# Score sums in four column groups on 32-token blocks, and a rearranged start, in a two-layer HGRN2/Fourier kernel

## The chip, the cores and the metric

One core of a Trainium2 chip runs the whole program in one launch. The metric is the device time in microseconds (us), as the median over runs. The engines are PE (matrix multiply; the profile calls its weight loads PEld), DVE (vector), ACT (activation), POOL (general) and SP, which here only issues DMAs. Matmuls read SBUF and write PSUM; DVE and ACT read both.

## The reference, cut to what matters

512 latent tokens and 256 context tokens of width 1024 go through two layers. Layer 0 is a bidirectional gated linear recurrence with 16 heads of 128 channels:

```
h = rms_norm(x, norm_g) * (1 + scale) + shift          # shift, scale: silu(c) @ ada_w + ada_b
q = silu(p[0]);  f = lb + (1 - lb) * sigmoid(p[1:3])   # forward and backward gates
k = 1 - f;  g = log(f);  v = p[3];  z = p[4]           # p = h @ w_in, per head
scores[t, s] = sum_c q[t, c] * exp(b[t, c] - b[s, c]) * k[s, c]   for s <= t,  b = cumsum(g)
o[t] = sum_s scores[t, s] v[s] + (q[t] * exp(b[t])) @ S           # S: the state before the chunk
y = rms_norm(o_forward + o_backward) * silu(z) @ w_out
```

Layer 1 is a Fourier mixer, and a final norm ends the program. The change touches only the start of layer 0 and, of the scores, two parts in each head: the entries with s = t ("own") and those of the other token of a pair, s = t ^ 1 ("near"). Both are sums over the 128 channels of a product that DVE has made for each token: `ks` for own, `pn` for near.

## The kernel before, in words

**Precision.** Large products are made of three fp32r matmuls, hi*hi, lo*hi and hi*lo (`mm3`, lines 95 to 97). `split` (lines 56 and 57) makes the two parts: ACT copies to fp32r, DVE subtracts. Small matmuls (transposes, scores, states) are plain fp32, which the profile records as two instructions each.

**Start (lines 100 to 323).** SP issues, one after the other, `ident`, `vecs`, the gate bounds, the four tiles of `x` (`xs`, 512 KB each), then the eight modulation tiles (`ada_load(d)`: two halves `wa` of 512 KB each) with the first projection weights between them. `normalize(n)` scales a row tile: ACT squares and sums, POOL raises to -0.5, DVE multiplies. For each of eight channel tiles d: `ada_mm` multiplies `wa` by the two padded condition columns (`rp`), eight fp32 matmuls whose weights have 32 columns, so that four of them write four different groups of 32 PSUM partitions; ACT copies the result (`row`); `turn` transposes the rows (`tp`); `ada_cols` turns `row` into columns (`mp`), DVE adds biases (`acol`, `bcol`), and `modulate` makes `hlh` and `hll`, the two parts of h. Between these stand `product`s: the first head's four latent projections (`first`), as far as h and the weights are there. The order on PE, ACT and DVE in this part is the order of the code. After the eight steps the context rows are normalized, turned and modulated into `hc` in the same way, with the fourth projection between them.

**Heads (lines 332 to 605).** `projections` yields in the middle of each projection; at each yield `advance` moves the scan of the head before by one step, so that PE has projection matmuls (`pf`, `pq`, `pfc`, `vps`) between the steps of a scan. From here on a scheduler sets each engine's order. A scan has seven levels with block length h = 1, 2, 4 ... 64. At level `lev` PE multiplies `kk` by `z4` for four token tiles (`gp`, line 529), DVE then multiplies `z4` by the decays of that level (line 537, two instructions), ACT packs the next `kk` (line 492), and DVE writes the level's entries from `gp` into the score matrix `am` under a mask (line 553). At level 6 ACT copies two 64-row blocks instead (lines 550 and 551). After the levels `am` is the weight of the matmuls that make the head's output.

The two parts that change: `parts` splits `ks` and `pn` into hi and lo (ACT and DVE), and `summed` multiplies each by a 128x128 matrix of ones on PE, two fp32r matmuls of 512 columns, which gives every PSUM partition the sum of every token. DVE multiplies the first by the identity into `am` (line 543) at level 1, and copies the second under the mask of level 0 (line 546) at level 2. PSUM tiles of scores come from a pool of two buffers (`psG`).

Of the kernel before, what the change touches and what calls it, by code (L numbers as in the profile page):

```python
# [7 lines left out]
F32 = mybir.dt.float32  # L8
# [6 lines left out]
P = 128  # L15
D = 1024
KT = D // P
T = 512
# [14 lines left out]
def hgrn_fourier_kernel(ctx: ExitStack, tc: tile.TileContext, a):  # L33
# [77 lines left out]
    def ada_load(d):  # L111
        wa[d] = []
        for j in range(2):
            h = KT // 2
            if d < 4:
                w = py.tile([P, h, 256], F32, tag=f"yp{2 * d + j}", name=f"wa{d}_{j}")
            else:
                w = p0.tile([P, h, 256], F32, name=f"wa{d}_{j}")
            nc.sync.dma_start(out=w, in_=a["ada_a"][d][:, j * h:(j + 1) * h, :])
            wa[d].append(w)  # L120

    for n in range(NT):
        nc.sync.dma_start(out=xs[:, n, :], in_=a["x"][n * P:(n + 1) * P, :])
    ada_load(0)
    masks = pc.tile([P, 7, P], U8, name="masks")
    ones = pc.tile([P, 256], F32, name="ones")
# [5 lines left out]

    vp = psM("vp")
# [26 lines left out]
    lp = psM("lp")  # L160
    pe.transpose(lp[:, :32], lmx, ident[:32, :32])
    lbc = pc.tile([P, 32], F32, name="lbc")
    v.tensor_copy(lbc, lp[:, :32])
    omlb = pc.tile([P, 32], F32, name="omlb")
    v.tensor_scalar(out=omlb, in0=lbc, scalar1=-1.0, scalar2=1.0, op0=ALU.mult, op1=ALU.add)
# [112 lines left out]
    with tc.manual_schedule(engines={mybir.EngineType.PE, mybir.EngineType.Activation, mybir.EngineType.DVE}):  # L278
# [17 lines left out]
        for n in range(NTC):  # L296
            nc.sync.dma_start(out=xs[:, NT + n, :], in_=a["ctx"][n * P:(n + 1) * P, :])
        for n in range(NT):
            normalize(n)
        todo = {2: [(0, 0), (1, 0)], 3: [(0, 1), (1, 1), (2, 0), (2, 1)]}  # L300
        for d in range(KT):
            ada_mm(d)
            turn(d, 0)
            for j, k in todo.get(d, [(j, d - 2) for j in range(3)] if d > 3 else []):
                product(j, k)
            ada_cols(d)
            modulate(d, 0)
            if d < 3:
                W.halves(d)
        W.halves(3)  # L310
        for j in range(3):
            product(j, KT - 2)
        for n in range(NT, NT + NTC):
            normalize(n)
        for j in range(3):
            product(j, KT - 1)
        for d in range(KT):
            turn(d, 1)
            modulate(d, 1)
            product(3, d)  # L320
    mraw = p0.tile([P, 7, P], F32, tag="junk", name="mraw")
    nc.sync.dma_start(out=mraw, in_=a["masks"])
    g.tensor_copy(masks, mraw)

# [128 lines left out]
    def scan(i, fl, z4, fc, q, zs):  # L453
# [42 lines left out]
        def parts(pr, name):  # L496
            hi = pw.tile([P, T], F32R, tag="yh", name=f"{name}h{i}", bufs=2)
            lo = pw.tile([P, T], F32R, tag="yh", name=f"{name}l{i}", bufs=2)
            split(hi, lo, pr)
            return hi, lo  # L500

        def summed(hl, name):
            gp = psG(f"{name}p{i}")
            pe.matmul(gp, ones_r, hl[0], start=True, stop=False)
            pe.matmul(gp, ones_r, hl[1], start=False, stop=True)
            return gp.rearrange("p (n t) -> p n t", n=NT)
# [15 lines left out]
        for lev in range(7):  # L522
# [17 lines left out]
            if lev == 0:  # L540
                own = parts(ks, "gd")
            elif lev == 1:
                v.tensor_tensor(out=am, in0=summed(own, "gd"), in1=ident.unsqueeze(1).broadcast_to([P, NT, P]), op=ALU.mult)
                near = parts(pn, "gn")
            elif lev == 2:
                v.copy_predicated(am, level_mask(0), summed(near, "gn"))
            if lev > 0:
                g3 = gp.rearrange("p (n t) -> p n t", n=NT)
                if lev == 6:
                    s.activation(am[:64, :, 64:], g3[:64, :, 64:], AF.Copy)  # L550
                    s.activation(am[64:, :, :64], g3[64:, :, :64], AF.Copy)
                else:
                    v.copy_predicated(am, level_mask(lev), g3)  # L553
# [425 lines left out]
```

## Time and profile before

| | us |
|---|---|
| median of 3 runs | 1215.77 |
| lowest, highest | 1214.56, 1216.39 |
| the profiled execution's own time | 1213.96 |
| its span in the trace | 1212.2 |
| PE busy in the span | 1181.1 (97%) |
| DVE, ACT busy | 801.0 (66%), 548.8 (45%) |
| PE on the chain that ended last | 92% |
| DMA mean | 98 GB/s |

The span is cut into stages roughly so: start to 66 us, heads to 860 us, then the output projection of layer 0, the second layer and the end. A row of the page's list of groups gives line, engine, operation, tiles and shapes, then busy time and mean duration of one in ns, then the idle time of the engine before them and what ended it. A row of the timeline gives start, duration from the first to the last of merged instructions, engine, line, operation, tiles and count; in brackets the idle time before it and what ended it. PE's durations are modelled with overlap, so that the distance from start to start is what a matmul costs in a stream.

### The profile page before, as it was taken

The numbers are of one execution on the slowest core, as the hardware profiler recorded it, in microseconds if no ns is written. First come the engines' busy times: TensorE is split into PE (matmuls) and PEld (weight loads), VectorE is DVE, ScalarE is ACT, GpSimd is POOL, SyncE is SP. The second block draws the span as 40 slices with busy tenths as digits, with TensorE's granted clock in tenths as the row PEclk, the third lists the DMA queues.
The fourth block names the chain that finished last, engine by engine and source line by source line (L and its number), as shares of the span: only waits on it lengthen the run. The fifth ranks groups of instructions, "written<-read, shape, count | busy, mean of one in ns | idle before, by whom it ended". The sixth has DMA issues, their size and how long they took to land.

```text
span 1212.2 us, 18500 instructions
## 1 busy us (share of the span) xinstructions
PE 1181.1 (97%) x7450; PEld 1052.4 (87%) x7450; DVE 801.0 (66%) x1292; ACT 548.8 (45%) x1040; POOL 35.3 (3%) x69
## 2 busy tenths in 40 slices
PE   5989999999999999999999999999999999999997
PEld 3689899899889989989988988997888998988885
DVE  5484766786686586687658557558676856668554
ACT  4455444554453453445445345355556533333322
POOL 1000000000000000000000000000000000000000
PEclk9999999999999999999999999999999999999999
DMA  9411222232331332242221121113545313333221
GB/s 357 183 36 53 70 71 87 91 102 70 104 110 52 118 105 87 69 128 86 68 70 53 38 66 54 36 53 105 166 174 180 102 52 127 114 108 122 87 87 69
DMA packets 33671, 118.49 MB, mean 98 GB/s; under 512 B 3879, under 2 KB 4144, under 8 KB 33586
## 3 DMA queue, kind: packets, MB, share of 16 engines
q1 hardware_dynamic: 33586, 117.32, 29.7%
q8 instruction: 58, 0.95, 0.3%
q14 instruction: 27, 0.22, 0.1%
HBM read 115.20 MB, written 2.10 MB: 97 GB/s over the span
## 4 chain that ended last, share of the span: by engine, by line
PE 92%; DMA 3%; DVE 2%; ACT 1%; issue 1%; POOL 0%; SPq 0%; DVEq 0%; POOLq 0%; ACTq 0%
PE gp L529 7%; PE pq L95 5%; PE pq L96 5%; PE pq L97 5%; PE pf L95 4%; PE pf L97 4%; PE pf L96 4%; PE vps L97 4%; PE vps L95 4%; PE vps L96 4%; PE pfc L95 3%; PE pfc L96 3%; PE pfc L97 3%; PE o0a L97 2%; PE o0a L95 2%; PE o0a L96 2%
## 5 line engine op out<-in xcount | busy, mean ns | idle before, releaser
L57 DVE TENSOR_TENSOR wl<-wr,wh 128x1024 fp32r<-128x1024 f32 x140 | 170.6, 1219 | 99.9 <-ACT wh L56 99.8
L56 ACT ACTIVATE wh<-wr 128x1024 fp32r<-128x1024 f32 x140 | 148.0, 1057 | 177.7 <-issue 53.3
L537 DVE TENSOR_TENSOR z<-z,tt 128x512 f32<-128x512 f32 x192 | 123.8, 686 | 85.0 <-PE gp L529 81.6
L529 PE MATMUL gp<-z,kk 128*128 128x128 f32 x768 | 102.8, 277 | 2.1 <-ACT kk L492 1.9
L529 PEld LDWEIGHTS gp<-z,kk 128*128 128x128 f32 x768 | 97.8, 191 | 6.8 <-ACT kk L492 2.9
L95 PE MATMUL pf<-hlh,wh 128*128 128x512 f32 x240 | 97.6, 407 | 0.0
L95 PE MATMUL pq<-hlh,wh 128*128 128x512 f32 x240 | 97.0, 404 | 0.0
L492 ACT ACTIVATE kk<-z 128x512 f32<-128x512 f32 x96 | 61.8, 643 | 72.1 <-DVE z L537 72.0
L97 PE MATMUL pf<-hlh,wl 128*128 128x512 f32 x240 | 94.3, 393 | 0.0
L97 PE MATMUL pq<-hlh,wl 128*128 128x512 f32 x240 | 93.8, 391 | 0.0
L96 PE MATMUL pf<-hll,wh 128*128 128x512 f32 x240 | 93.8, 391 | 0.0
L96 PE MATMUL pq<-hll,wh 128*128 128x512 f32 x240 | 93.7, 390 | 0.0
L95 PE MATMUL pfc<-hc,wh 128*128 128x256 f32 x256 | 74.3, 290 | 3.0 <-ACT fl L402 3.0
L95 PE MATMUL vps<-wh,hlh 128*128 128x256 f32 x256 | 73.5, 287 | 0.0
L96 PE MATMUL pfc<-hc,wh 128*128 128x256 f32 x256 | 72.4, 283 | 0.0
L97 PE MATMUL vps<-wh,hll 128*128 128x256 f32 x256 | 72.4, 283 | 0.0
L96 PE MATMUL vps<-wl,hlh 128*128 128x256 f32 x256 | 72.4, 283 | 0.0
L97 PE MATMUL pfc<-hc,wl 128*128 128x256 f32 x256 | 72.4, 283 | 0.0
L553 DVE COPY_PREDICATED am<-masks,gp 128x512 f32<-128x512 uint8 x80 | 58.8, 735 | 0.3
L348 DVE SCALAR_TENSOR_TENSOR acc<-ar,scol,acc 128x1024 f32<-128x1024 f32 x30 | 38.5, 1283 | 26.3 <-DMA ar<-ada_r 26.2
L97 PEld LDWEIGHTS pf<-hlh,wl 128*128 128x128 f32 x240 | 45.1, 188 | 10.1 <-issue 0.2
L97 PEld LDWEIGHTS pq<-hlh,wl 128*128 128x128 f32 x240 | 45.0, 188 | 9.8
(267 smaller groups left out, 3019.5 us busy)
## 6 DMA issues: line engine op xcount, KB each, us to landing
wr<-hg_w SPq DMA_DIRECT2D x64, 512.0 KB, 3.5
ar<-ada_r SPq DMA_DIRECT2D x32, 512.0 KB, 3.7
wr<-ft_w SPq DMA_DIRECT2D x32, 512.0 KB, 3.8
wr<-hg_wout SPq DMA_DIRECT2D x29, 512.0 KB, 3.5
wa<-ada_a SPq DMA_DIRECT2D x16, 512.0 KB, 10.4
wr<-hg_v SPq DMA_DIRECT2D x16, 512.0 KB, 3.5
wr<-ft_wout SPq DMA_DIRECT2D x16, 512.0 KB, 3.5
xs<-x SPq DMA_DIRECT2D x4, 512.0 KB, 4.5
```

Of the source, the lines that this page charges most:

```text
L56: s.activation(hi, src, AF.Copy)
L57: v.tensor_tensor(out=lo, in0=src, in1=hi.bitcast(F32), op=ALU.subtract)
L95: pe.matmul(out, lh, rh, start=first, stop=False)
L96: pe.matmul(out, lh, rl, start=False, stop=False)
L97: pe.matmul(out, ll, rh, start=False, stop=last)
L348: v.scalar_tensor_tensor(out=acc, in0=raw, scalar=scol[:, 0, k:k + 1], in1=acc, op0=ALU.mult, op1=ALU.add)
L492: s.activation(view(kk, 0, [[2 * h, T // (2 * h)], [h, 2], [1, h]]), view(z4, 2 * T, [[2 * h, T // (2 * h)], [T + h, 2], [1, h]]), AF.Copy)
L529: pe.matmul(gp[:, n * P:(n + 1) * P], kk[:, n * P:(n + 1) * P], view(z4, n * P, dims), start=True, stop=True)
L537: v.tensor_tensor(out=za, in0=za, in1=ta, op=ALU.mult)
L553: v.copy_predicated(am, level_mask(lev), g3)
```

## The change

Three parts of the start and one of the heads:

- `ada_load(0)` is issued ahead of the four tiles of `x`. `ada_mm(0)` stands ahead of the rows' normalization, and 26 fp32r matmuls of ones by ones (`keep_warm`), whose results nobody reads, are put around it on PE. The gate bounds (`lp`) move behind the second `ada_mm`.
- The context rows are normalized in steps 6 and 7 of the loop instead of behind it; their transposes are issued two steps ahead, the first two ahead of the last nine products.
- Two small masks are made on POOL (`own_m`, `near_m`, 128x32: the sum of a 128x128 mask's four column blocks).
- In each head `sums` replaces `parts` and `summed`: for each of `ks` and `pn` four fp32 matmuls with 32 columns of ones as weights. The j-th takes the j-th block of 32 tokens of each of the four token tiles (128 columns) and writes PSUM partitions 32j to 32j+31, so that partition p holds the sums of the 32 tokens of p's own block. DVE masks these into `amc` (128 x 4 x 32; one multiplication and one copy under a mask), ACT copies four blocks of 32 partitions into `am`. No split is needed. Besides, level 5's copy under a mask on DVE becomes four copies of 32x128 elements on ACT.

```
+    ada_load(0)
     for n in range(NT):
         nc.sync.dma_start(out=xs[:, n, :], in_=a["x"][n * P:(n + 1) * P, :])
-    ada_load(0)
...
+    def keep_warm(n, name):
+        wp = psG(name)
+        for j in range(n):
+            pe.matmul(wp, ones_r, view(ones_r, 0, [[0, 4], [1, P]]), start=True, stop=True)
+
+    keep_warm(4, "warm0")
...
+        keep_warm(12, "warm1")
+        ada_mm(0)
+        keep_warm(10, "warm2")
         for n in range(NT):
             normalize(n)
...
-        W.halves(3)
+            if d > 5:
+                normalize(NT + d - 6)
         for j in range(3):
             product(j, KT - 2)
-        for n in range(NT, NT + NTC):
-            normalize(n)
+        W.halves(3)
+        for d in range(2):
+            turn(d, 1)
         for j in range(3):
             product(j, KT - 1)
         for d in range(KT):
-            turn(d, 1)
             modulate(d, 1)
             product(3, d)
+            if d + 2 < KT:
+                turn(d + 2, 1)
...
-        def summed(hl, name):
-            gp = psG(f"{name}p{i}")
-            pe.matmul(gp, ones_r, hl[0], start=True, stop=False)
-            pe.matmul(gp, ones_r, hl[1], start=False, stop=True)
-            return gp.rearrange("p (n t) -> p n t", n=NT)
+        def sums(srcs):
+            gp = psG(f"cs{i}")
+            for e, src in enumerate(srcs):
+                for j in range(4):
+                    pe.matmul(gp[32 * j:32 * j + 32, e * P:(e + 1) * P], ones[:, :32],
+                              view(src, 32 * j, [[P, NT], [1, 32]]), start=True, stop=True)
+            return [view(gp, e * P, [[32, NT], [1, 32]]) for e in range(2)]
...
-            if lev == 0:
-                own = parts(ks, "gd")
-            elif lev == 1:
-                v.tensor_tensor(out=am, in0=summed(own, "gd"), in1=ident.unsqueeze(1).broadcast_to([P, NT, P]), op=ALU.mult)
-                near = parts(pn, "gn")
-            elif lev == 2:
-                v.copy_predicated(am, level_mask(0), summed(near, "gn"))
+            if lev == 1:
+                own, near = sums((ks, pn))
+                amc = sp.tile([P, NT, 32], F32, tag="amc", name=f"amc{i}")
+                v.tensor_tensor(out=amc, in0=own, in1=own_m.unsqueeze(1).broadcast_to([P, NT, 32]), op=ALU.mult)
+                v.copy_predicated(amc, near_m.unsqueeze(1).broadcast_to([P, NT, 32]), near)
+                for j in range(4):
+                    c = slice(32 * j, 32 * j + 32)
+                    s.activation(am[c, :, c], amc[c], AF.Copy)
             if lev > 0:
-                if lev == 6:
-                    s.activation(am[:64, :, 64:], g3[:64, :, 64:], AF.Copy)
-                    s.activation(am[64:, :, :64], g3[64:, :, :64], AF.Copy)
+                if lev >= 5:
+                    for j in range(0, P, h):
+                        c = slice(j, j + h)
+                        o = slice(j ^ h, (j ^ h) + h)
+                        s.activation(am[c, :, o], g3[c, :, o], AF.Copy)
```

What this does to the engines' orders is shown at three places. The first is PE at the program's start, where `vp` transposes the condition vectors, `rp` is `ada_mm`, `tp` the transposed rows and `mp` the modulation's columns. Before:

```order
L134 MATMUL vp<-ident,vrow 128x65
L161 MATMUL lp<-ident,lmx 128x32
L196 MATMUL rp_194<-wa_0_84,spad 32x256 x4
L196 MATMUL rp_194<-wa_1_86,spad 32x256 x4
L215 MATMUL tp_0_205<-ident,xs 128x128 x4
L204 MATMUL mp_210<-sel,row_203 128x2 x2
```

And the same place of the changed kernel:

```order
L138 MATMUL warm_97<-ones_r 128x512 x4
L138 MATMUL warm_177<-ones_r 128x512
L142 MATMUL vp<-ident,vrow 128x65
L138 MATMUL warm_177<-ones_r 128x512 x11
L206 MATMUL rp_190<-wa_0_80,spad 32x256 x4
L206 MATMUL rp_190<-wa_1_82,spad 32x256 x4
L138 MATMUL warm_201<-ones_r 128x512 x10
L225 MATMUL tp_0_232<-ident,xs 128x128 x4
L214 MATMUL mp_237<-sel,row_199 128x2 x2
```

Five unread matmuls now stand ahead of `vp`, eleven ahead of the first `rp` and ten behind it; `lp` has moved out of these rows.

The second place is PE at the end of the start, where `first` are the last products of the eight steps (`wh`, `wl`) and the fourth projection's (`wz`), and `tp_1` are the transposed context rows. Before:

```order
L95 MATMUL first_311<-hlh,wh_285 128x512
L96 MATMUL first_311<-hll,wh_285 128x512
L97 MATMUL first_311<-hlh,wl_286 128x512
L215 MATMUL tp_1_497<-ident,xs 128x128 x2
L95 MATMUL first_504<-hlh,wz_465 128x512
L96 MATMUL first_504<-hll,wz_465 128x512
L97 MATMUL first_504<-hlh,wz_466 128x512
L215 MATMUL tp_1_508<-ident,xs 128x128 x2
```

In the changed kernel (seven more rows of products stand behind these, up to the first `wz`):

```order
L97 MATMUL first_342<-hlh,wl_317 128x512
L225 MATMUL tp_1_519<-ident,xs 128x128 x2
L225 MATMUL tp_1_522<-ident,xs 128x128 x2
L95 MATMUL first_299<-hlh,wh_246 128x512
L96 MATMUL first_299<-hll,wh_246 128x512
```

The first two context transposes now stand ahead of the last nine products instead of behind them.

The third place is level 1 and 2 of head 8's scan, on DVE and ACT. DVE before, from the decays of level 1 to those of level 3 (`gdp` and `gnp` are the own and near sums, `gnl` the low part of `pn`):

```order
L537 TENSOR_TENSOR z_8_3996<-z_8_3996,tt_0_4456 128x2x128x2 x2
L543 TENSOR_TENSOR am_4442<-gdp_4492,ident 128x512
L57 TENSOR_TENSOR gnl_4497<-pn_4446,gnh_4496 128x512
L553 COPY_PREDICATED am_4442<-masks,gp_1_4483 128x512
L537 TENSOR_TENSOR z_8_3996<-z_8_3996,tt_1_4501 128x2x64x4 x2
L546 COPY_PREDICATED am_4442<-masks,gnp_4544 128x512
L553 COPY_PREDICATED am_4442<-masks,gp_2_4535 128x512
```

DVE in the changed kernel:

```order
L559 TENSOR_TENSOR z_8_4056<-z_8_4056,tt_0_4515 128x2x128x2 x2
L565 TENSOR_TENSOR amc_4560<-cs_4551,own_m 128x128
L566 COPY_PREDICATED amc_4560<-near_m,cs_4551 128x128
L578 COPY_PREDICATED am_4505<-masks,gp_1_4542 128x512
L559 TENSOR_TENSOR z_8_4056<-z_8_4056,tt_1_4568 128x2x64x4 x2
L578 COPY_PREDICATED am_4505<-masks,gp_2_4602 128x512
```

And ACT in the changed kernel, up to the last `kk` of that head (before, the rows are the same but for `gnh` ahead of `kk_4` and without the two rows of `am`):

```order
L518 ACTIVATE kk_4_4549<-z_8_4056 128x512
L569 ACTIVATE am_4505<-amc_4560 32x4x32 x4
L413 ACTIVATE vt_4430<-vps_2_4517 128x512
L518 ACTIVATE kk_8_4609<-z_8_4056 128x512
L499 ACTIVATE kct_4504<-ctp_4651 128x512
L518 ACTIVATE kk_16_4646<-z_8_4056 128x512
L56 ACTIVATE wh_4700<-wr_4435 128x1024
L413 ACTIVATE vt_4430<-vps_4_4614 128x512
L56 ACTIVATE wh_4822<-wr_4441 128x1024
L518 ACTIVATE kk_32_4689<-z_8_4056 128x512
L576 ACTIVATE am_4505<-gp_5_4719 32x4x32 x4
L518 ACTIVATE kk_64_4726<-z_8_4056 128x512
```

DVE's copy under level 1's mask now stands behind ACT's four copies into the same `am`, and level 5's four copies stand ahead of the last `kk` on ACT.

More of the change, by code (lines that the diff above doesn't have):

```diff
@@ L120, in ada_load @@
             wa[d].append(w)
+    ada_load(0)
     for n in range(NT):
         nc.sync.dma_start(out=xs[:, n, :], in_=a["x"][n * P:(n + 1) * P, :])
-    ada_load(0)
     masks = pc.tile([P, 7, P], U8, name="masks")
+    near_m = pc.tile([P, 32], U8, name="near_m")
+    own_m = pc.tile([P, 32], F32, name="own_m")
     ones = pc.tile([P, 256], F32, name="ones")
@@ L159, in hgrn_fourier_kernel, with lower_bounds @@
     v.tensor_tensor(out=lmx, in0=le[:, 0, :], in1=lmx, op=ALU.mult)
-    lp = psM("lp")
-    pe.transpose(lp[:, :32], lmx, ident[:32, :32])
     lbc = pc.tile([P, 32], F32, name="lbc")
-    v.tensor_copy(lbc, lp[:, :32])
     omlb = pc.tile([P, 32], F32, name="omlb")
-    v.tensor_scalar(out=omlb, in0=lbc, scalar1=-1.0, scalar2=1.0, op0=ALU.mult, op1=ALU.add)
+    def lower_bounds():
+        lp = psM("lp")
+        pe.transpose(lp[:, :32], lmx, ident[:32, :32])
+        v.tensor_copy(lbc, lp[:, :32])
+        v.tensor_scalar(out=omlb, in0=lbc, scalar1=-1.0, scalar2=1.0, op0=ALU.mult, op1=ALU.add)
     def rstd_of(ss, n, width, pool, name):
@@ L301, in hgrn_fourier_kernel @@
         for d in range(KT):
-            ada_mm(d)
+            if d > 0:
+                ada_mm(d)
+            if d == 1:
+                lower_bounds()
             turn(d, 0)
@@ L323, in hgrn_fourier_kernel @@
     g.tensor_copy(masks, mraw)
+    for t, src in ((own_m, ident), (near_m, mraw[:, 0, :])):
+        msum = p0.tile([P, 32], F32, tag="msum", name=f"msum{t.name}", bufs=2) if t is near_m else own_m
+        g.tensor_tensor(out=msum, in0=src[:, 0:32], in1=src[:, 32:64], op=ALU.add)
+        for j in (64, 96):
+            g.tensor_tensor(out=msum, in0=msum, in1=src[:, j:j + 32], op=ALU.add)
+        if t is near_m:
+            g.tensor_copy(near_m, msum)
     st_start.close()
@@ L494, in side @@
             return kk
[L496 to L500, printed above, removed]
-        def summed(hl, name):
-            gp = psG(f"{name}p{i}")
-            pe.matmul(gp, ones_r, hl[0], start=True, stop=False)
-            pe.matmul(gp, ones_r, hl[1], start=False, stop=True)
-            return gp.rearrange("p (n t) -> p n t", n=NT)
+        def sums(srcs):
[5 more added lines that the diff above has]
+            return [view(gp, e * P, [[32, NT], [1, 32]]) for e in range(2)]
         def level_mask(lev):
```

## The prediction

> **What bounds the kernel now.** I read the page's busy times, then its chain, then PE's waits behind the start.
>
> ```profile
> span 1212.2 us, 18500 instructions
> PE 1181.1 (97%) x7450; PEld 1052.4 (87%) x7450; DVE 801.0 (66%) x1292; ACT 548.8 (45%) x1040; POOL 35.3 (3%) x69
> PE 92%; DMA 3%; DVE 2%; ACT 1%; issue 1%; POOL 0%; SPq 0%; DVEq 0%; POOLq 0%; ACTq 0%
> PE gp L529 <- ACT kk L492: 1.9, 2, 1.6
> ```
>
> PE carries 92% of the chain. The last row is PE's longest entry in the list of waits from 72 us on: of all the heads it waited for ACT 1.9 us in two places. So in the heads a matmul removed from PE shortens the run by what it costs in the stream, and the 3 us per head that DVE loses are worth nothing by themselves. The start is another matter: there DMA, ACT and PE take turns. The sum is made against the profiled execution, 1213.96 us (1.8 around its span of 1212.2). The median of the runs is 1.8 above that, and the forecast is given as a median.
>
> **Sums on PE, what goes.** PE's rows around both sums of head 1:
>
> ```profile
> 135.96 1.12 PE L529 MATMUL gp<-z,kk 128*128 128x128 f32 x8
> 136.83 0.49 PE L504 MATMUL gdp<-gdh,ones_r 128*128 128x512 f32 x1
> 137.16 0.40 PE L505 MATMUL gdp<-gdl,ones_r 128*128 128x512 f32 x1
> 137.40 0.28 PE L95 MATMUL pfc<-hc,wh 128*128 128x256 f32 x1
> ...
> 140.26 1.06 PE L529 MATMUL gp<-z,kk 128*128 128x128 f32 x8
> 141.07 0.47 PE L504 MATMUL gnp<-gnh,ones_r 128*128 128x512 f32 x1
> 141.39 0.39 PE L505 MATMUL gnp<-gnl,ones_r 128*128 128x512 f32 x1
> 141.61 0.40 PE L95 MATMUL pf<-hlh,wh 128*128 128x512 f32 x1
> ```
>
> From start to start the own pair takes 0.57 us (136.83 to 137.40), the near pair 0.54. In each the first is 0.10 longer than the second (0.33 and 0.24; 0.32 and 0.22): it is the first fp32r matmul behind an fp32 one, and the next projection matmul will pay that instead. So 1.11 - 0.20 = 0.91 us per head go, 16 x 0.91 = 14.6 us.
>
> **Sums on PE, what comes.** Eight fp32 matmuls, two instructions each, with 32-column weights in four column groups. `rp` has that form, with 256 columns; it is shown warm, in three cuts of the timeline and with the transpose behind it:
>
> ```profile
> 39.06 0.42 PE L196 MATMUL rp<-wa,spad 128*32 128x256 f32 x4
> 39.30 0.82 PE L196 MATMUL rp<-wa,spad 128*32 128x256 f32 x11
> 39.73 0.40 PE L196 MATMUL rp<-wa,spad 128*32 128x256 f32 x4
> 40.06 0.33 PE L215 MATMUL tp<-ident,xs 128*128 128x128 f32 x1
> ```
>
> Sixteen instructions start in waves of four: the first at 39.06, the last at 39.73, so a wave takes 0.67 / 3 = 0.22 us, and the four groups do run together. From the last wave to the next 128-column matmul it is 0.33, that is 0.11 more than a wave. With 128 columns a wave is half, 0.11, which is also what an instruction of `gp` takes (0.81 us for eight, 140.26 to 141.07). Four waves are 0.44, the step out of column groups 0.11. The step in has no clear row; it lies between nothing and the 0.11 of the step out, and I take the middle, 0.05. That makes 0.60 us per head, 9.6 in all. The ends: 0.44 (no steps, 7.0 in all) and the whole of `rp`, 1.00 (39.06 to 40.06, 16.0 in all). I take a value near the lower end, since columns, and not the count of instructions, set the waves in both rows above. So PE gains 14.6 - 9.6 = 5.0 us, with ends of +1.4 and -7.6 on the time.
>
> The Trainium skill (TensorEngine Tiling (Array Packing), Key Properties) says that a change of tiling mode drains TensorE. The trace agrees with 0.11 us at the exit of `rp`; two such drains per head, 16 x 0.22 = 3.5 us as an estimate, would leave 4.1 of the 5.0.
>
> **What DVE and ACT do with it.** DVE loses two subtractions, two full-width writes of `am` and one copy under a mask; ACT loses two splits and gets eight small copies. The danger is the order: DVE's copy at level 1 now waits for four ACT copies, and `z` of level 2 is behind it. Head 8:
>
> ```profile
> 479.73 1.30 DVE L537 TENSOR_TENSOR z<-z,tt 128x512 f32<-128x512 f32 x2 [3.16 <-PE gp L529]
> 481.06 0.63 ACT L492 ACTIVATE kk<-z 128x512 f32<-128x512 f32 x1 [0.53 <-DVE z L537]
> 482.14 0.73 DVE L553 COPY_PREDICATED am<-masks,gp 128x512 f32<-128x512 uint8 x1
> 482.80 1.05 PE L529 MATMUL gp<-z,kk 128*128 128x128 f32 x8
> 483.96 1.29 DVE L537 TENSOR_TENSOR z<-z,tt 128x512 f32<-128x512 f32 x2 [1.08 <-PE gp L529]
> ...
> 497.45 0.63 ACT L492 ACTIVATE kk<-z 128x512 f32<-128x512 f32 x1 [3.12 <-DVE z L537]
> 498.51 1.05 PE L529 MATMUL gp<-z,kk 128*128 128x128 f32 x8
> 500.96 0.38 ACT L551 ACTIVATE am<-gp 64x256 f32<-64x256 f32 x1
> 501.35 0.28 ACT L482 ACTIVATE st<-s 128x128 f32<-128x128 f32 x1
> 501.52 0.27 ACT L483 ACTIVATE st<-s 128x128 f32<-128x128 f32 x1
> ```
>
> `z` ends at 481.03; two DVE instructions on 128 elements at some 0.28 (the row of `st`, same size) end at 481.6. ACT's `kk` ends at 481.69, its four copies, 0.17 apart (the two `st` rows) to 0.28, at 482.4 to 482.8; DVE's masked copy of 0.73 ends by 483.6. `z` of level 2 waits for `gp` until 483.96 anyway: hidden, with 0.4 us to spare. At level 5 four copies, 0.7 to 1.1 us, stand ahead of the last `kk`, beside the 1.29 of DVE's `z`, and that `kk` (ends 498.08) has 0.43 us before PE asks for it. In odd heads, whose ACT also does gates there, I expect a few tenths here and there: 0.3 us in all. The ends: -1.9 (both waits above vanish) and +8 (second rival).
>
> **The start, front.** Rows in order of time, from the timeline:
>
> ```profile
> 10.05 1.06 ACT L186 ACTIVATE junk<-xs 128x1024 f32<-128x1024 f32 x1
> 12.76 0.75 DVE L188 TENSOR_SCALAR xs<-xs,rstd_x 128x1024 f32<-128x1024 f32 x1 [0.71 <-POOL rstd_x L170]
> 13.29 0.20 PEld L196 LDWEIGHTS rp<-wa,spad 128*32 128x32 f32 x8 [0.96 <-DMA wa<-ada_a]
> 15.21 0.85 PE L204 MATMUL mp<-sel,row 128*128 128x2 f32 x4
> 27.20 1.06 ACT L56 ACTIVATE wh<-wr 128x1024 fp32r<-128x1024 f32 x1 [0.83 <-DMA wr<-hg_w]
> 29.58 0.50 PE L97 MATMUL first<-hlh,wl 128*128 128x512 f32 x1 [0.53 <-DVE wl L57]
> ```
>
> DMAs land in order of issue; the second half of `wa` 0 lands at 13.29. After the swap that place is the last row tile's. Its way through ACT, POOL and DVE takes what it took (10.05 to 13.51), so it is scaled at about 16.3, a transpose follows, and `mp` starts at 16.5 instead of 15.21: 1.3 us later. The chain `mp`, DVE, ACT's `hlh`, `wh`, `row` repeats in d = 0, 1, 2 and comes to `wh` of the third weight, where ACT stood 0.83 us for its DMA. So up to 0.5 us of the delay passes on to PE at 29.58, and up to 0.9 if the transposes and `rp` run at the cold rate. From there PE is full to the end of the eight steps in both. No gain is possible here: the third weight's DMA keeps its place in the queue. I take +0.5, between 0 and +1.5. The 26 unread matmuls lie in time that PE waits for DMA; they cost nothing and, since PE has almost nothing to do between their end and 16 us, buy nothing.
>
> **The start, end.**
>
> ```profile
> 48.37 0.77 ACT L224 ACTIVATE h<-tp,bcol,acol 128x512 f32<-128x512 f32 x1
> 51.16 1.06 ACT L186 ACTIVATE junk<-xs 128x1024 f32<-128x1024 f32 x1
> 51.64 0.39 PE L97 MATMUL first<-hlh,wl 128*128 128x512 f32 x1
> 54.35 0.33 PE L215 MATMUL tp<-ident,xs 128*128 128x128 f32 x1 [1.08 <-DVE xs L188]
> 62.96 0.43 DVE L228 TENSOR_TENSOR hc<-h,hc 128x256 fp32r<-128x256 f32 x1
> 63.88 0.42 DVE L228 TENSOR_TENSOR hc<-h,hc 128x256 fp32r<-128x256 f32 x1
> 66.39 0.39 PE L95 MATMUL pfc<-hc,wh 128*128 128x256 f32 x1 [3.03 <-ACT fl L402]
> 55.00:60.00 5.00, 5.00 (x22) 3.91 (x21) 3.52 (x8) 2.02 (x5) 0.93 (x1) 0.70 0.52 167
> ```
>
> The last context row is squared at 51.16 and reaches PE at 54.35, 3.2 later. In the new order ACT squares it behind the last `h`, at about 49.2, so PE has it at 52.4, 2.0 earlier; but nine products of 0.23 (2.1 us), done before by 51.9, now stand behind that transpose, and PE waits some 3 us ahead of it instead of 2.4. The context transposes then run ahead of their use. With a warm PE: 52.4, three transposes 0.4, nine products 2.1, the first three of the fourth projection 0.7, then five steps of 0.92 (62.96 to 63.88) to the last transposes at 60.2, their own time, ACT's copy and DVE's pair together 2.3: the last `hc` ends at 62.5, 1.8 before 64.3. With a cold PE it ends at 63.7, for the granted clock was 0.70 in the five microseconds behind the old gap (last row: its last three figures are clock, DMA share and GB/s), which is 1.5 us lost, most of it in this stretch. The new gap is as long, so cold is likelier: -0.9 on average, between -1.8 and 0. What follows to 66.39 (ACT's first gates) is the same. With the +0.5 of the front the start gives -0.4, between -1.8 and +1.5.
>
> The Trainium skill (TensorE: Matmul & The Clock Gate, Part 1) has the clock halved after an idle window of about 3.4 us that runs freely, and restored after a busy one; the 0.70 above agrees. By that rule the unread matmuls warm PE by 8 us, and the wait to 16 us cools it again.
>
> **The sum.** -14.6 + 9.6 + 0.3 - 0.4 = -5.1 us: 1208.9 for an execution like the profiled one, 1215.77 - 5.1 = 1210.7 as a median.
>
> **Rivals.**
> - The start gains all it can (PE warm through both gaps, -1.8) and the sums cost 0.50: -1.8 - 6.6 = -8.4, near 1207.5. For it: PE kept its full clock through the 3.0 us gap before 66.39. Against: the gap before 54.35, shorter, cost it.
> - ACT becomes the bound, and the kernel is slower. In the eight odd heads ACT has gates and weight splits (1.06 each) between the copies. If each copy takes the 0.38 of L551, four take 1.5 at level 5 and at level 1, where room is about 1.0 each; with one split in between, a head loses some 0.5 at both places, 8 x 1.0 = 8. Then -14.6 + 9.6 + 8 - 0.4 = +2.6, 1218.4. It decides from 0.33 us lost per head on. Against: 0.17 between the `st` rows, and ACT is 45% busy.
> - The column groups do not run together, because all four use the same ones: eight matmuls one by one are 8 x 0.22 = 1.76 us per head, 16 x (1.76 - 0.91) = +13.6, 1229. Against: `rp`.
> - The front loses its 1.5 and a cold window more (1.5 us): -5.0 + 0.3 + 3.0 = -1.7, 1214, no measurable change.
>
> **Chances.** My forecast 0.57, the first rival 0.15, ACT 0.10, groups one by one 0.05, the front 0.13. 0.2% is 2.4 us, about what a measurement of this kernel can tell from no change. Faster by more: 0.57 + 0.15 + 0.02 of the front = 0.74; within: 0.11 of the front + 0.06 of ACT = 0.17; slower: 0.04 + 0.05 = 0.09. Leaving out the lower half of the first rival, the one-by-one case and the worse part of ACT, the range is 1206.8 to 1215.8.
>
> **What will show it.** Right: `cs` in four waves about 0.11 apart and some 0.6 us from its first start to the next projection; PE's waits for `kk` still near 2 us; DVE some 45 us less busy in all; `mp` of d = 0 near 16.5, the second weight's wait at 29.6 to 30.1, `pfc` at 65 to 66. Wrong: `cs` over 0.9 us, waits of `gp` for `kk` in odd heads, or the first `pfc` before 64 or behind 67.5.

## Result and the profile after: 0.4% slower

The changed kernel takes 1219.74 us (median of 6 runs, 1217.69 to 1220.03), the kernel before took 1214.20 beside it: a ratio of 1.0039, 95% interval 1.0026 to 1.0052. That is 5 us slower where 5 us faster was forecast. The profiled execution after took 1217.69, its span is 1215.9; it is the fastest of the six.

From the page of the kernel after (span; busy time by engine; the chain that ended last by engine), to be held against the first three rows of the prediction:

```profile
span 1215.9 us, 18949 instructions
PE 1185.7 (98%) x7668; PEld 1050.6 (86%) x7668; DVE 763.1 (63%) x1244; ACT 565.8 (47%) x1136; POOL 37.5 (3%) x76
PE 82%; DVE 7%; DMA 5%; ACT 3%; issue 2%; POOL 1%; SPq 0%; DVEq 0%; POOLq 0%; ACTq 0%
```

The work went where it was forecast: DVE has 38 us less (45 forecast), ACT 17 more. But PE lost ten points of the chain to DVE, DMA and ACT. PE's waits from 72 us on name the place (engine, tile and line that waited, what for: us in total, times, longest):

```profile
PE gp L551 <- DVE amc L566: 4.9, 4, 1.9
PE gp L551 <- ACT kk L518: 1.1, 2, 0.6
```

Four waits for `amc`; the trace of before has no wait of PE in these places. They lie in heads 3, 5, 7 and 9. The time from the first `gp` of a head to the first `gp` of the next, worked out from the starts of these rows in the traces (before, after, and two of the experiments below: e2 has the heads of before behind the new start, e13 those of after with one thing moved):

| head | 3 | 5 | 7 | 9 | 11 | 13 | 12 | 14 |
|---|---|---|---|---|---|---|---|---|
| before | 43.79 | 43.73 | 43.67 | 43.67 | 43.67 | 43.67 | 54.53 | 51.28 |
| after | 45.19 | 45.11 | 44.79 | 46.88 | 43.62 | 43.63 | 54.42 | 51.18 |
| e2 | 45.53 | 43.67 | 43.67 | 44.64 | 43.67 | 43.67 | 54.53 | 51.29 |
| e13 | 43.62 | 43.62 | 43.61 | 43.62 | 43.62 | 43.62 | 54.41 | 51.17 |

So against undisturbed heads the four lose 1.57 + 1.49 + 1.18 + 3.26 = 7.5 us. The rest of the result is what the sums gain and what the start loses, both below.

**What holds PE up.** A side job, `ada_rest`, which the prediction did not look at, runs beside the heads: at every third step it loads 512 KB of `ada_r`, and DVE adds the block loaded before to a sum (`acc`, 32 times). Head 3 in the timeline of the kernel after:

```profile
237.51 0.28 DVE L565 TENSOR_TENSOR amc<-cs,own_m 128x128 f32<-128x128 f32 x1
239.36 1.28 DVE L374 SCALAR_TENSOR_TENSOR acc<-ar,scol,acc 128x1024 f32<-128x1024 f32 x1 [1.56 <-DMA ar<-ada_r]
240.56 0.29 DVE L566 COPY_PREDICATED amc<-near_m,cs 128x128 f32<-128x128 uint8 x1
240.89 1.26 ACT L569 ACTIVATE am<-amc 32x128 f32<-32x128 f32 x4 [2.62 <-DVE amc L566]
241.00 1.13 PE L551 MATMUL gp<-z,kk 128*128 128x128 f32 x8 [1.17 <-DVE amc L566]
```

Between the two writes of `amc`, which are neighbours in the code, the scheduler has put an `acc`. DVE works in order, so it stands 1.56 us for a DMA, adds for 1.28, and only then reads `cs` for the last time; `gp` of level 2 needs the PSUM buffer of `cs` and waits 1.17 us. The chain of waits of the same kernel shows the DMA behind it (start, duration, what):

```profile
234.96 4.31 DMA ar<-ada_r
239.36 1.28 DVE acc L374
241.00 1.13 PE gp L551 x8
```

In the kernel before, the data of the same step lands at nearly the same time (`acc` at 239.55) and DVE waits for it too (0.48 us), but behind the write that PE needs:

```profile
238.34 0.73 DVE L553 COPY_PREDICATED am<-masks,gp 128x512 f32<-128x512 uint8 x1
239.55 1.29 DVE L348 SCALAR_TENSOR_TENSOR acc<-ar,scol,acc 128x1024 f32<-128x1024 f32 x1 [0.48 <-DMA ar<-ada_r]
```

The old heads are not proof against this wait. In the trace of e2 (old heads, new start) DVE stands 2.50 us for such a DMA in head 3, ahead of `z`, and PE waits for what follows:

```profile
246.12 1.28 DVE L365 SCALAR_TENSOR_TENSOR acc<-ar,scol,acc 128x1024 f32<-128x1024 f32 x1 [2.50 <-DMA ar<-ada_r]
249.40 1.13 PE L546 MATMUL gp<-z,kk 128*128 128x128 f32 x8 [1.58 <-ACT kk L509]
```

But with the accumulations where they were, heads 3, 5, 7 and 9 together lose 6.8 to 7.9 us in each of the five traces with the new sums (after, e1, e3, e4, e7; against 43.62 a head) and 0.0 to 2.8 us in the six with the old ones (before, e2, e6, e12, e14, e15; against 43.67).

**The sums themselves.** Head 12, first the kernel before, then the kernel after: levels 1 to 3 of `gp` with the sums between.

```profile
678.61 1.13 PE L529 MATMUL gp<-z,kk 128*128 128x128 f32 x8
679.48 0.49 PE L504 MATMUL gdp<-gdh,ones_r 128*128 128x512 f32 x1
682.91 1.06 PE L529 MATMUL gp<-z,kk 128*128 128x128 f32 x8
687.13 1.05 PE L529 MATMUL gp<-z,kk 128*128 128x128 f32 x8
```

```profile
685.53 1.13 PE L551 MATMUL gp<-z,kk 128*128 128x128 f32 x8
686.59 0.42 PE L526 MATMUL cs<-ks,ones 128*32 128x128 f32 x8
686.83 0.40 PE L526 MATMUL cs<-pn,ones 128*32 128x128 f32 x8
690.14 1.06 PE L551 MATMUL gp<-z,kk 128*128 128x128 f32 x8
693.91 1.06 PE L551 MATMUL gp<-z,kk 128*128 128x128 f32 x8
```

From level 1 to 2 it is 4.61 instead of 4.30, from 2 to 3 3.77 instead of 4.22. The near pair's 0.45 is gone as forecast (0.44). The four waves of `cs` start 0.24 apart by pairs, so the column groups do run together, and the next projection starts 0.58 behind the first `cs` (some 0.6 was forecast); but from the first `gp` to `cs` it is 1.06 instead of 0.87, that is 0.19 for the step into column groups, where 0.05 was put. Together with 0.10 (odd heads) or 0.03 (even heads) that come back behind level 6, a head gains 0.05 (odd) or 0.1 (even), not 0.31.

Head 15 gains more than that. Before, PE waited ahead of its first `gp`; after, a step of the output projection (`o0a`) stands there:

```profile
828.10 1.23 PE L529 MATMUL gp<-z,kk 128*128 128x128 f32 x8 [1.58 <-ACT kk L492]
```

```profile
834.37 0.39 PE L97 MATMUL o0a<-wh,o0y 128*128 128x512 f32 x1
834.76 1.23 PE L551 MATMUL gp<-z,kk 128*128 128x128 f32 x8
```

From its first to its last `gp` head 15 takes 20.3 us instead of 23.3, in every kernel with the new sums. Not all of that is gain: the eight instructions of the context's state (`s`) have moved behind the last `gp`. At the next step that both kernels share, the first `ktp` of head 15, 2.1 us are left of it (26.93 us from the first `gp` before, 24.83 after). Over the 15 heads before it the first `gp` goes from 0.54 later than before to 6.66 later, which without the 7.5 of the stalls is a gain of 1.4. So in these traces the new sums are worth about 1.4 us in 15 heads and 2.1 in the last, 3.5 in all, where the prediction had 5.0.

**The start.** The timeline after, beside the rows of before in the prediction (`mp` at 15.21, the low matmul at 29.58):

```profile
16.60 0.85 PE L214 MATMUL mp<-sel,row 128*128 128x2 f32 x4
21.64 1.93 PE L206 MATMUL rp<-wa,spad 128*32 128x256 f32 x16 [0.39 <-DVE lbc L174]
30.84 0.50 PE L97 MATMUL first<-hlh,wl 128*128 128x512 f32 x1 [0.65 <-DVE wl L57]
```

`mp` is 1.39 late, as forecast (1.3); then 0.4 are lost to a copy of the moved gate bounds, whose PSUM buffer `rp` of step 2 needs, and 1.26 arrive at the third weight, not 0.5. At the first `pfc` of head 0 (66.95 instead of 66.39) the new end has won 0.7 of that back, and the first `gp` of head 0 is 0.54 late. This trace is a lucky one, though: its clock record has PE at half rate for 10.24 us from 15.1 us on. In e2, e4 and e18, with the same start, it is 13.65 us, and the first `gp` of head 0 comes 3.3 to 3.7 us later than in before.

### The profile page after: what moved, and what is told of

Read it like the earlier page. It is cut to its first block, busy times and chain, and to the rows that moved or that the text cites. A ratio compares the mean times of both kernels' runs of the same rounds, so it can differ in the third digit from the quotient of the medians.

```text
span 1215.9 us, 18949 instructions
## 1 busy us (share of the span) xinstructions
PE 1185.7 (98%) x7668; PEld 1050.6 (86%) x7668; DVE 763.1 (63%) x1244; ACT 565.8 (47%) x1136; POOL 37.5 (3%) x76
## 4 chain that ended last, share of the span: by engine, by line
PE 82%; DVE 7%; DMA 5%; ACT 3%; issue 2%; POOL 1%; SPq 0%; DVEq 0%; POOLq 0%; ACTq 0%
PE gp L551 7%; PE vps L95 4%; PE vps L97 4%; PE vps L96 4%; PE pf L97 4%; PE pf L95 4%; PE pf L96 4%; PE pq L95 3%; PE pq L97 3%; PE pq L96 3%; DMA ar<-ada_r 3%; PE o1a L95 2%; PE o1a L96 2%; PE o1a L97 2%; PE o0a L97 2%; PE o0a L95 2%
## 5 line engine op out<-in xcount | busy, mean ns | idle before, releaser
L578 DVE COPY_PREDICATED am<-masks,gp 128x512 f32<-128x512 uint8 x64 | 47.2, 738 | 20.4 <-ACT am L569 20.4
L374 DVE SCALAR_TENSOR_TENSOR acc<-ar,scol,acc 128x1024 f32<-128x1024 f32 x30 | 38.5, 1283 | 32.0 <-DMA ar<-ada_r 31.8
```

What stands on the lines that cost most here:

```text
L374: v.scalar_tensor_tensor(out=acc, in0=raw, scalar=scol[:, 0, k:k + 1], in1=acc, op0=ALU.mult, op1=ALU.add)
```

## Experiments

Each was timed in turn with the kernel before on one chip; ratios are to that, with 95% intervals. The medians of the kernel before were 1214.11 (e1 to e4), 1213.77 (e5 to e8), 1213.95 (e9 to e12), 1214.05 (e13 to e16) and 1213.80 us (e17, e18).

### The two halves apart: e1, e2

e1 is the kernel before with the masks and the new heads; e2 has the new start and the old heads.

> The heads of the changed kernel with the start of the kernel before. Theory (DVE's queue): the loss lies in heads 3, 5, 7 and 9, where an accumulation of the late modulation weights (acc, waiting for its DMA ada_r) stands on DVE between the two writes of amc; in the profile these four heads cost 7.2 us and the rest of the change in the heads gains some 4, so this kernel is about 3 us slower than before: 1217, with the same four stalls. Rival (the start costs it): without the new start the sums gain, 1212 to 1213.

> The start of the changed kernel with the heads of the kernel before. Theory: the start gives 0.3 us in the profile and up to 2 in the median, 1214.5 to 1216.5. Rival (the start costs it): 1218 to 1220.

e1: 1215.82 us, 1.0010 (1.0000 to 1.0021). e2: 1217.35, 1.0025 (1.0014 to 1.0036). Both medians are above before (e1's interval reaches down to 1.0000), and the two ratios add up to 1.0035, near the 1.0039 of the whole. e2's 1.0025, 3.0 us, is not the start's alone: in its trace the first `gp` of head 0 is 3.7 us late, and heads 3 and 9 lose another 2.8. e1 shows the same four waits as after, with its old start:

```profile
PE gp L535 <- DVE amc L550: 4.5, 4, 2.0
```

### Is it the PSUM buffer, or DVE's queue? e3, e4

```
-            gp = psG(f"cs{i}")
+            gp = psM(f"cs{i}")          # e3: cs from another pool
```

e4 keeps the steps of `ada_rest` from standing behind levels 0 to 2 of a scan.

> The changed kernel with the sums' PSUM tile taken from the pool of the transposes and states (M) instead of the pool of the scores (G). Rival (a PSUM buffer is what holds gp of level 2): the four stalls go, 1212 to 1213. Theory (DVE's queue): gp of level 2 starts on time, but z of level 2 is behind acc all the same, so the wait moves to gp of level 3: 1218 to 1220.

> The changed kernel with the accumulation steps of the late modulation weights put off while a scan stands behind its levels 0, 1 or 2, so that none stands between the two writes of amc on DVE; PE's order is the same. Theory (DVE's queue): the four stalls go, 7 us less than the changed kernel, 1212 to 1213, and faster than before by 1 to 2. Rival (the start, or the column groups as such): 1219 to 1220.

e3: 1219.87, 1.0049 (1.0034 to 1.0064). e4: 1219.74, 1.0043 (1.0027 to 1.0059). Neither helped, and the waits only changed their name. In e4 the `acc` left the gap between the writes of `amc` and stood one place earlier, ahead of `z` of level 1, with a second one ahead of `z` of level 2:

```profile
239.85 1.28 DVE L374 SCALAR_TENSOR_TENSOR acc<-ar,scol,acc 128x1024 f32<-128x1024 f32 x1 [3.15 <-DMA ar<-ada_r]
241.05 1.29 DVE L559 TENSOR_TENSOR z<-z,tt 128x512 f32<-128x512 f32 x2
244.85 1.26 DVE L374 SCALAR_TENSOR_TENSOR acc<-ar,scol,acc 128x1024 f32<-128x1024 f32 x1
246.04 1.28 DVE L559 TENSOR_TENSOR z<-z,tt 128x512 f32<-128x512 f32 x2
248.04 1.16 PE L551 MATMUL gp<-z,kk 128*128 128x128 f32 x8 [1.08 <-ACT kk L518]
```

PE's waits in e4 are then `gp` for `kk`, 5.3 us in 7 places, and the four heads lose 6.8 us (7.7 in e3, 7.5 after). The buffer of `cs` was one way of the wait to PE; `z` and `kk` are another.

### The accumulation on another engine: e5, e8

```
-                    v.scalar_tensor_tensor(out=acc, in0=raw, scalar=scol[:, 0, k:k + 1], in1=acc, ...)
+                    g.tensor_scalar(out=raw, in0=raw, scalar1=scol[:, 0, k:k + 1], scalar2=None, op0=ALU.mult)
+                    g.tensor_tensor(out=acc, in0=acc, in1=raw, op=ALU.add)
```

e5 is the kernel after with this; e8 the kernel before with this, the new heads and the new end of the start.

> The kernel after, with one thing changed: the accumulation of the ada_r rows (32 times one DVE instruction of 1.28 us that first waits for its DMA) is made on POOL, as a product and a sum. So nothing on DVE waits for ada_r any more. Theory DVE's queue (in heads 3, 5, 7 and 9 the accumulation holds z or the copies of amc back until its DMA lands, and PE runs dry): the first gp of head 10 comes some 5 to 7 us earlier against the first gp of head 3 than in the kernel after (there +6.7 between the two against the kernel before), and the time falls from 1219.7 to 1213 to 1215. Rival ACT (the copies of amc on ACT, or kk behind them, are what is late in those heads): the four heads still lose 1.2 to 3 us each and the time stays at 1219 to 1220. Rival shared port (POOL's two passes slow DVE's copies beside them): DVE's z grows from 1.29 to over 1.6 and the time is 1217 or more. The start is as in the kernel after in all three.

> The kernel before with the new sums in the heads, the new order of the context part, and the accumulation of ada_r on POOL; the front (x first, no unread matmuls, lower bounds ahead of the eight steps) is as before. Theory DVE's queue and front: the end of the start gains 0.7, the heads 0.15 each (2.4 in all), head 15 another 2 to 3: 1208 to 1210. Rival ACT: the four heads lose their 5 to 7 us, 1214 to 1216. Rival sums (the column groups gain nothing in the stream): 1213 to 1214.

e5: 1241.66, 1.023 (1.0216 to 1.0244); e8: 1238.66, 1.0201 (1.0185 to 1.0217). A miss: some 22 us slower than after. In e5's trace POOL takes 3.15 us for the product and 2.57 for the sum (groups: busy us, mean ns, idle time before and what ended it):

```profile
L374 POOL TENSOR_SCALAR ar<-ar,scol 128x1024 f32<-128x1024 f32 x30 | 94.6, 3152 | 160.9 <-DMA ar<-ada_r 121.3 <-DVE pn L538 12.1 <-DVE z L559 10.1
L375 POOL TENSOR_TENSOR acc<-acc,ar 128x1024 f32<-128x1024 f32 x30 | 77.2, 2574 | 2.4
```

DVE's `z` (duration in ns as minimum, median and maximum) has the median it had (685 after), but 14 `z` of this line take 1.5 to 2.9 us, where the longest takes 0.70 after:

```profile
L559 DVE TENSOR_TENSOR z<-z,tt x192: 657/685/2908, 82.5 to 883.3; 128x512 f32<-128x512 f32 x192
```

Twelve of the 14 begin while POOL makes a sum, and end 0.54 to 0.55 us behind it, as the second of these two `z` does; every `z` of the line that begins within a sum is among them:

```profile
616.27 3.52 DVE L559 TENSOR_TENSOR z<-z,tt 128x512 f32<-128x512 f32 x2 [0.56 <-PE gp L551]
616.36 2.88 POOL L375 TENSOR_TENSOR acc<-acc,ar 128x1024 f32<-128x1024 f32 x1
```

Besides, `rstd_o` of the heads' output stands behind the accumulation in POOL's queue, with ACT and PE behind it (4.15 us here, twice):

```profile
328.73 1.04 POOL L180 TENSOR_TENSOR rstd_o<-rstd_o,nhalf 128x4 f32<-128x4 f32 x1
329.80 1.14 ACT L621 ACTIVATE os<-op,rstd_o 128x128 f32<-128x128 f32 x4 [8.17 <-POOL rstd_o L180]
330.22 1.25 PE L625 MATMUL otp<-ident,os 128*128 128x128 f32 x4 [4.15 <-ACT os L621]
```

So e5 does not tell on the theory; it moved the accumulation to a worse place.

### The accumulation in the even heads: e9 to e11, e13, e16 to e18

In the kernel after an `acc` stands between the writes of `amc` in four odd heads and in no even one. The cover is no shorter in odd heads: from level 1 to 2 PE has 24 projection matmuls (`pfc` in odd heads, `vps` in even ones) and takes 4.61 us in undisturbed heads of both kinds. `ada_rest` was given steps of even heads alone.

```
+        hd = made_n - len(scans)                                  # the head whose scan runs
-        if step > 30 and step % 3 == 0:
+        if step > 30 and step % 2 == 0 and hd % 2 == 0:           # e9, e10, e11
+        if step > 20 and step % 3 > 0 and hd % 2 == 0:            # e13, e16, e17, e18
             next(side_work, None)
```

e9 is after with the first form, e10 before with the new heads and it, e11 before with it alone. e13, e17 and e18 are, in this order, new heads alone, nothing else, and all of after, with the second form, which ends in head 10 (the last `acc` at 600.5 us in e13's trace, at 578.0 before); e16 is e13 with the new end of the start.

> The kernel after, with the ada_r rows loaded and accumulated (still on DVE, 32 times 1.28 us) only at steps of the even heads, so that no accumulation stands on DVE in the first levels of heads 3, 5, 7 and 9. Theory DVE's queue: those four heads lose nothing against the kernel before (each +0.2 at most, where the kernel after lost 1.3 to 3.1), and the time falls by 4 to 7 us, from 1219.7 to 1213 to 1216; what is left is the start. Rival ACT (copies of amc, kk): the four heads still lose 1.2 to 3 us each, 1219 to 1220. Rival other heads (the waits move to heads 4, 6, 8): the losses show there and the time is 1217 or more.

> The kernel before with the new sums and masks in the heads, its own old start, and the accumulations in the even heads alone. Theory DVE's queue: 15 heads gain 0.15 each, the stalls of 5 to 7 us are gone and head 15 gives 2 to 3 more: 1209 to 1211, faster than both. Rival ACT: as the sums with the old start did before, 1215 to 1216. Rival (head 15's gain came only because the late heads had lost time to give back): 1212 to 1213.

> The kernel before with only the accumulations moved to the even heads: a control. All theories: its four odd heads had no stall, so nothing is to be gained there, 1213 to 1215; were it 1210 or less, the gain of the run above would be the move's own and not the end of a stall that the sums made.

> As the run with the sums, the old start and the accumulations in the even heads, but with two of three steps of those heads used, so that the last accumulation stands in head 10, as in the kernel before, and the gates' matmuls lie in the heads again and not behind head 15. Theory DVE's queue, with a price of 2 to 3 us for accumulations that reach into the late heads (the control with them alone took 1218.1): 1210 to 1211.5. Rival (even heads 4, 6 and 8 now hold so many accumulations that PE waits there): losses of 1 to 2 us in these heads, 1213 to 1215. Rival (the sums gain nothing, the gain of the run before was scatter): 1213.5 to 1214.5.

> As the first run of this call, with the new order of the context part added. The end alone measured -0.2 on the kernel before, so: within 0.5 of the first run of this call, 1209.5 to 1211.5 by the theory; by the rivals named there 1213 to 1215.

> Control of the run with sums and accumulations up to head 10 (1211.0): the kernel before with only that move of the accumulations. If the sums gain the 5.0 us of the prediction once nothing waits in odd heads: 1215 to 1216.5. If the move itself is the gain: 1211 to 1212. If it is worth nothing in a kernel that had no stall there, and the sums gain 3: 1213.5 to 1214.5.

> The whole change, with the accumulations in the even heads up to head 10. If heads and start add up: 1211.0 + 3.0 (the new start alone) = 1214, within 1; 1218 or more would mean that the stalls need the new start as well.

| | us | ratio to before (95%) |
|---|---|---|
| after | 1219.74 | 1.0039 (1.0026 to 1.0052) |
| e9: after, even heads | 1215.72 | 1.0014 (1.0005 to 1.0022) |
| e18: after, even heads up to 10 | 1213.54 | 0.9998 (0.9990 to 1.0007) |
| e10: new heads, even heads | 1213.38 | 0.9991 (0.9981 to 1.0001) |
| e13: new heads, even heads up to 10 | 1211.05 | 0.9978 (0.9966 to 0.9990) |
| e16: e13 with the new end | 1212.04 | 0.9978 (0.9970 to 0.9987) |
| e11: even heads alone | 1218.09 | 1.0035 (1.0022 to 1.0048) |
| e17: even heads up to 10 alone | 1216.85 | 1.0023 (1.0013 to 1.0034) |

The four heads lose nothing any more (row e13 of the first table), with the same copies on ACT, the same PSUM buffers and the same number of accumulations. Head 3 of e13, at the place shown of after:

```profile
238.49 0.28 DVE L549 TENSOR_TENSOR amc<-cs,own_m 128x128 f32<-128x128 f32 x1
238.81 0.30 DVE L550 COPY_PREDICATED amc<-near_m,cs 128x128 f32<-128x128 uint8 x1
239.15 1.27 ACT L553 ACTIVATE am<-amc 32x128 f32<-32x128 f32 x4
240.65 1.06 PE L535 MATMUL gp<-z,kk 128*128 128x128 f32 x8
```

DVE still waits in e13 for `ada_r`, 29.6 us in 23 places (31.8 in 18 after), but in the heads PE then waits only three times, 0.28 to 0.44 us, for a `kk`. In its heads 2, 8 and 10 an `acc` does stand in level 1, with 0.5 to 0.7 us of waiting, but behind both writes of `amc`, and from level 1 to 2 these heads take 4.61 like the others.

The controls e11 and e17 say that the move alone costs 3 to 4 us by ratio, so it is no gain of its own: it ends stalls. Part of the cost shows in the even heads 4 to 10, which together take 226.7 us in e13 instead of 224.9 after, and 226.8 in e17 instead of 225.4 before; where the rest lies was not found. With the accumulations at equal places the new heads are worth 0.9978 against 1.0023, 5.4 us by ratio, give or take 1.9 (e10 against e11: 0.9991 and 1.0035, 5.3). The traces say less: from the first `gp` of head 0 to the first `ktp` of head 15 e13 takes 774.7 us and e17 777.8, 3.1 less. Some 2 us of the 5.4 may be the clock: the median granted clock of e13's runs is 0.997, that of e17's 0.9945, and among the runs of before 0.001 less goes with 0.7 to 1.0 us more; this is an estimate.

The parts add up: the whole change with the accumulations moved, e18, is at 0.9998, within the intervals of e13 with the 1.0025 of e2. e13 and e16 beat both kernels, by 2.7 us against before.

### The start piece by piece: e6, e7, e12, e14, e15

e6: before with the new end (context part) alone. e7: after without the 26 unread matmuls. e12: before with ada tile 0 ahead of `x`, and `ada_mm(0)` ahead of the normalization. e14: before with the unread matmuls alone. e15: before with the gate bounds moved into step 1 alone.

> The kernel before with the new order of the context part alone (context rows normalized behind steps 6 and 7, its transposes two tiles ahead, the halves of the fourth weight behind the first nine products); the front, the sums and the masks are as before. Theory front (what the start loses comes from the front: ada tile 0 first, the transpose of the lower bounds at step 1; the end gains 0.7 as the traces of before and after give it): 1213 to 1213.7, the first pfc some 0.7 us earlier than before. Rival end (the loss sits in the new end, by its cold windows at 55 and 68 us): 1216 to 1217.5, the first gp of head 0 two to three us later than before.

> The kernel after without its 26 unread matmuls. Prediction as made (they cost nothing and buy nothing): 1219.7, within 0.6. Rival harm (they put the chip's clock on a phase whose half-rate windows reach to 25 to 28 us): the first third-projection matmul, 30.8 to 32.2 us with them, stands at 30.5 to 31 and the time is 1217.5 to 1218.5. Rival help (without them step 0 and the window from 5 us on run at half rate for longer): 1221 to 1222.

> The kernel before with ada tile 0 loaded ahead of x and its products made ahead of the normalization; no unread matmuls, lower bounds and context part as before. Theory swap (the last row tile of x reaches PE 1.3 us later, and all of it passes on): the first mp of step 0 at 16.5 instead of 15.2, the third weight's first low matmul at 30.6 to 30.9 instead of 29.6, and 1215 to 1216. As predicted (0.5 passes on): 30.1, 1214 to 1214.5. Rival lower bounds (the start's loss comes from their transpose at step 1 and the unread matmuls): no change in the time, 1213.8 within 0.6.

> The kernel before with the 26 unread matmuls alone (4 ahead of the first transpose, 22 ahead of the normalization), nothing else changed. As predicted for them: no change, within 0.6 of before. Rival harm (the kernel after is 1.6 us slower with them than without): 1215 to 1216, with one half-rate window more between 50 and 75 us or a half-rate stretch that reaches further than 25 us. Rival help: 1212.5 to 1213.

> The kernel before with the transpose of the lower bounds and their copy moved into step 1 alone. In the trace after, rp of step 2 waited 0.4 us for that copy and the transpose itself took 0.2. Theory (it passes on): the third weight's first low matmul 0.3 to 0.6 later, 1214.2 to 1214.6. As predicted (nothing): within 0.3 of before.

| | us | ratio to before (95%) |
|---|---|---|
| e2: the whole new start | 1217.35 | 1.0025 (1.0014 to 1.0036) |
| e12: ada tile 0 first | 1215.55 | 1.0015 (1.0006 to 1.0024) |
| e15: gate bounds in step 1 | 1215.36 | 1.0004 (0.9995 to 1.0012) |
| e14: unread matmuls | 1215.10 | 1.0002 (0.9990 to 1.0015) |
| e6: new end | 1213.54 | 0.9998 (0.9989 to 1.0007) |
| e7: after without unread matmuls | 1218.01 | 1.0026 (1.0015 to 1.0037) |

Only the swap is resolved: 1.8 us. In its trace `mp` of step 0 starts at 17.2, 2.00 later than before, and the third weight's low matmul at 31.12, 1.54 later:

```profile
17.21 0.85 PE L204 MATMUL mp<-sel,row 128*128 128x2 f32 x4
31.12 0.50 PE L97 MATMUL first<-hlh,wl 128*128 128x512 f32 x1 [0.64 <-DVE wl L57]
```

The end alone gains nothing that is resolved, against the 0.7 that was expected: in its trace the first `pfc` is 0.6 earlier than before, but the first `gp` of head 0 0.75 later, behind a half-rate window from 65.4 to 68.8 us. The unread matmuls alone neither help nor harm as far as the interval tells. Taken out of the whole they are worth 1.0039 against 1.0026, but these intervals overlap: whether they cost 1.6 us in the company of the swap stays open. The four single ratios sum to 1.0019, within the intervals of the 1.0025.

What e14 does show is what they do. Windows of 5 us (start and end, length, busy us and instructions of PE, PEld, DVE, ACT and POOL, granted clock, DMA share, GB/s), with two `mp` of its timeline:

```profile
15.00:20.00 5.00, 4.01 (x38) 2.23 (x40) 3.04 (x5) 2.72 (x5) 0.00 (x0) 0.76 1.02 407
20.00:25.00 5.00, 5.00 (x30) 3.75 (x26) 2.13 (x4) 1.99 (x4) 0.00 (x0) 0.55 1.03 415
```

```profile
13.79 0.61 PE L210 MATMUL mp<-sel,row 128*128 128x2 f32 x4
32.03 0.85 PE L210 MATMUL mp<-sel,row 128*128 128x2 f32 x4
```

Step 0 is 1.4 us earlier than before, at the full clock. Then PE waits for `wa` (1.03 us ahead of `rp` at 15.43), the clock is halved from 17.6 to 24.5 us, and `mp` of step 3 comes 1.4 later than before (30.61). Its runs spread from 1210.6 to 1217.9, as wide as those of e2, which has these matmuls too.

## Why the prediction was wrong, step by step

- **DVE's and ACT's stalls (+0.3, "hidden, with 0.4 us to spare"): the step that failed.** Against undisturbed heads it was +7.5. The head that was read, 8, is an even one, without an accumulation in its first levels; the step counted what ACT puts between DVE's instructions and not what the scheduler puts there on DVE itself. That DVE stands for `ada_r` was in the trace of before, and that an `acc` stands between the two writes of `amc` in exactly four heads could be read in the changed kernel's order. Its upper end of +8 held the loss, but by another mechanism, so that was luck.
- **The rival of ACT as the bound** had the size (1218.4) nearly right, the place half right (four of the eight odd heads) and the cause wrong: ACT's four copies at level 1 take 1.26 after and 1.27 us in e13, where PE waits for none of them.
- **The sums (-14.6 + 9.6 = -5.0): the right sign, too large by the traces.** They came out at -3.5 in the traces of before and after and at -3.1 in those of e13 and e17; the -5.4 by ratio has an interval that reaches to -3.5. They are made up otherwise than forecast: the step into column groups costs 0.19 and not 0.05, up to 0.10 comes back behind level 6, and 2.1 of the gain lie in head 15, where the prediction had 0.3.
- **The drains of a tiling mode.** By the Trainium skill (TensorEngine Tiling (Array Packing), Key Properties) a change of mode drains TensorE; the 0.19 at the entry is in line with that and larger than the 0.11 that the prediction set as its bound. No run here shows that it is the drain.
- **The start's front (+0.5): wrong.** `mp` came 1.39 late (1.3 forecast), but the slack at the third weight took up less than the 0.8 that was reckoned: 0.46 of the 2.00 in e12, and 0.13 of the 1.39 after, where the gate bounds' copy, costed at nothing, holds PE up 0.4 more. The swap alone costs 1.8 us.
- **The start's end (-0.9): open.** PE's waits are much as forecast (2.7 us ahead of the context rows' transposes, 2.5 ahead of the first `pfc`), and up to the first `pfc` the end gains 0.7 after and 0.5 in e6; but e6's total gives 0.2, which is not resolved. In e6's trace a half-rate window stands behind each of the two waits.
- **The unread matmuls ("cost nothing and buy nothing"): right in sum**, as far as e14 resolves it, though they put step 0 1.4 us ahead and step 3 1.4 us behind. By the Trainium skill (TensorE: Matmul & The Clock Gate, Part 1) the clock is halved after an idle window of about 3.4 us that runs freely. The clock records of these traces agree in the length: the half-rate stretches inside the run last 3.41, 6.83, 10.24 or 13.65 us. The window ahead of one need not be wholly idle: PE was busy for 1.39 of the 3.41 us ahead of the stretch at 54.56 in before, and for 1.93 ahead of that at 948.85.

In sum, by the two traces: +0.54 (start, to the first `gp`) + 7.5 (stalls) - 3.5 (sums) - 0.8 (behind the heads, where the trace of before has a half-rate window at 948.9 and that of after none) = +3.7, the difference between the spans. The medians lie further apart, 4.7 us by ratio; the traced run is the fastest of its six, and the start varies by some 3 us with the clock.

## What to carry to other kernels

Before a wait is called hidden, read what else stands in that engine's queue in every variant of the loop: a side job fed by DMA that does little harm at one place of an in-order queue can hold up everything behind it at a place a few instructions earlier, here 1.2 to 3.3 us in each of four heads. Read the variant of the loop that holds the most side work, not the one that is easiest to read. Keeping a side job out of the gap between two writes that another engine waits for can be worth more than the change itself: here the choice of heads was worth 5 us by ratio between e18 and after. Putting it one place earlier (e4) was worth nothing.

## What the hardware showed that was not expected

- A sum on POOL holds DVE up. Beside it the same `z` takes up to 2.91 us instead of 0.69, and ends 0.55 us behind POOL's sum; beside the product most `z` keep their 0.69. The Trainium skill (SBUF — State Buffer, Who interferes with whom) calls the port pair that the two share an exclusive lock, which a DVE instruction with two SBUF inputs needs against a POOL one that reads SBUF; the twelve rows beside the sum agree, most of those beside the product do not.
- The granted clock in the first rows of a trace can be an absent record and not a full clock. Before shows 1.00 from 15 to 20 us, where `mp` took 0.85 us, but its clock records begin only at 23.8; after, the same `mp` takes 0.85 at a clock of 0.51:

```profile
15.00:20.00 5.00, 3.86 (x26) 2.31 (x26) 2.32 (x5) 2.00 (x3) 0.48 (x1) 0.51 1.02 388
```

- Where half-rate windows fall varies from run to run of one kernel: between 50 and 1200 us the trace of e10 has one, at 66.5, that of e17 one at 948.5, and that of before two, at 54.6 and 948.9. Runs of one kernel spread over 2 to 7 us, and the slower ones have the lower granted clock, so that a step of one microsecond needs the traces as well as the medians.
